# Gate of the feed-forward layers by the Silu table function, with the tokens' rstd moved to the last product

## The chip, the cores and the metric

The kernel runs on one core of a Trainium2 chip. A core has a matrix engine (TensorE; PE in the profile, PEld for its weight loads), a vector engine (VectorE, DVE), a table-function engine (ScalarE, ACT), a general engine (GpSimd, POOL), a sync engine (SP) and 16 DMA engines. Each engine works through its own instructions in order and waits for the others through semaphores. The metric is the device time of one execution in microseconds (us), the median of several executions.

## The reference, cut to what matters

Two hybrid attention layers come first. Then two layers of another kind follow, over 512 tokens of 1024 features, and the change is in their feed-forward parts:

```python
def swiglu(h, w1, w3, w2):
    return (jax.nn.silu(h @ w1) * (h @ w3)) @ w2
...
for l in range(DEPTH):                                   # DEPTH = 2
    x = x + 0.5 * swiglu(rmsnorm(x, ffn1_norm[l]), ffn1_w1[l], ffn1_w3[l], ffn1_w2[l])
    h = rmsnorm(x, mix_norm[l])
    ...                                                  # HGRN2 heads and a multiscale pool: "mix"
    x = x + mem_cross_attention(rmsnorm(x, xa_norm[l]), rmsnorm(mem, mem_norm[l]), ...)
    x = x + 0.5 * swiglu(rmsnorm(x, ffn2_norm[l]), ffn2_w1[l], ffn2_w3[l], ffn2_w2[l])
return rmsnorm(x, final_norm)
```

rmsnorm multiplies each token by rstd = 1 / sqrt(mean(x * x) + 1e-6) and each feature by a gain. The hidden width of a feed-forward part is 2816, which is 22 tiles of 128 features.

## The kernel before, in words

Activations lie feature-major: 128 features on the partitions, the 512 tokens on the free axis, so one activation tile is 128x512 and x is eight tiles. A dense product is three passes of TensorE (`mm3`, L296 to L298) over an exact split of both operands: a leading part ("hi", h) and the rest ("lo", l). Weights come in chunks by DMA (`wraw`); ScalarE copies out the leading part (`whi`, L287) and VectorE subtracts (`wlo`, L288), with two buffers of each. Three PSUM banks called `mm` collect sums of products, and a unit's sum is taken out of its bank ("evacuated") two units later.

The gain of a norm is applied when x is split for the next product: as a tile of x becomes final, `ready` has ScalarE write `xsh` (L262) and VectorE `xsl` (L263). The rstd is not known then. Its sum of squares passes through TensorE (L421) while the first products run, and `rsqrt` makes the value (Ln L440, Exp L441, Square L442 on ScalarE, then L443 and L444 on VectorE). It is multiplied into the products when they are evacuated. So the first evacuation of a stage waits for that chain, which sits in ScalarE's queue between conversions of weights.

A feed-forward part is `ffn`: two halves of 11 hidden tiles, each half w1 and w3 (22 units in turn, evacuated by `ev`), then w2 (8 units, `ev2`). Each evacuation of w1 gives a gate: si = ps * r on VectorE (L886), a clamp on GpSimd (L501), Exp, Ln, Exp on ScalarE (L504 to L506) for the sigmoid, then * r (L888) and the product with the sigmoid (L889) on GpSimd. The w3 product is multiplied with it on VectorE (L893) and split into `hh` and `hl`. There are 4 such parts of 22 gates, so 88 gates in all.

ScalarE holds one set of table functions at a time. A switch is an instruction of its own, ACT_TABLE_LOAD. The setup of this kernel fetches, at L597, a set that has both Ln and Exp, and nothing later needs another.

The stages, in us of the profiled execution: hybrid layers to 770; feed-forward 1 of layer 0 to 1137; mix to 1350; cross attention to 1510; feed-forward 2 to 1880; then for layer 1 to 2250, 2455, 2615 and 2977; the last norm to the end. The program order is made by a queue of units in which later units start before earlier ones are evacuated, and a scheduler (Tile) puts each engine's instructions in order. Work tiles come from a pool ("slot", 34 buffers).

Of the kernel before, what the change touches and what calls it, by code (L numbers as in the profile page):

```python
"""Two hybrid attention layers, then two HGRN2 / pool / cross-attention layers, on one core.

Activations live feature-major: features on the partitions, the 512 tokens on the free axis.
Dense products run on the tensor engine as float32r passes: an operand is split exactly into
a leading part of 12 significant bits and the rest, and three passes carry lead*lead, rest*lead
and lead*rest, which keeps the accuracy of a float32 product.
"""
# [23 lines left out]
EPS = 1e-6  # L31
# [5 lines left out]
# tiles of a tag get their room in program order, so work that runs at its own pace has a tag of its own  # L37
# [18 lines left out]
# engines of the steps that more than one can take: V(ector), P(ool), A(ctivation)  # L56
# [7 lines left out]
# ---------------------------------------------------------------- layout of the inputs (host)  # L64
def _chunks(w, c):
    """[K, M] -> [M/c, 128, K/128, c]"""
    k, m = w.shape
    return np.ascontiguousarray(w.reshape(k // P, P, m // c, c).transpose(2, 1, 0, 3))


def _cols(v):
    """[n*128] -> [128, n]"""
    return v.reshape(-1, P).T
# [37 lines left out]
def _constants():  # L111
    a = np.zeros((P, CONST.n), np.float32)

    def put(name, v):
        o, w = CONST.at[name]
        a[:, o:o + w] = v

    p = np.arange(P)[:, None]
    put("ident", np.eye(P))
    put("ones", 1.0)  # L120
    put("bd", (p // 64 == np.arange(P)[None] // 64))
    u = np.arange(512)[None]
    dist = p + 384 - u
    put("causal", np.where(dist >= 0, 0.0, BIG))
    cnt = ((dist >= 0) & (dist <= 128)) * 1 + ((dist >= 0) & (dist % 4 == 0)) * 1 + ((dist >= 0) & (dist % 16 == 0)) * 1
    put("dil", np.where(cnt > 0, -np.log(np.maximum(cnt, 1)), BIG))
    put("tri", (u >= p))
    put("reset", (u % 64 != 0))
    put("diag", p % 32 == np.arange(32)[None])
    t16 = np.arange(16)[None]  # L130
    put("pool", np.concatenate([1.0 / np.minimum(t16 + 1, w) for w in (2, 4, 8, 16)], 1))
    put("eps", EPS)
    # pairs s, t of 32 tokens in the two halves of a segment of 2 hs tokens
    lev = np.zeros((P, 5, 32), np.float32)
    s, t = np.arange(P)[:, None] % 32, np.arange(32)[None]
    for n, hs in enumerate((16, 8, 4, 2, 1)):
        lev[:, n] = (s // (2 * hs) == t // (2 * hs)) & (s % (2 * hs) < hs) & (t % (2 * hs) >= hs)
    sel = np.zeros((96, 8, P), np.float32)
    for h in range(8):
        for part in range(3):  # L140
            sel[32 * part + h, h] = 1.0
    return a, lev, sel


def _pack(i):
# [5 lines left out]
    # 8 frequencies x 16 blocks of 32 tokens  # L151
# [55 lines left out]
# ---------------------------------------------------------------- the program  # L207
class Prog:
# [9 lines left out]
    # tiles  # L218
# [34 lines left out]
    # exact split of float32 into two float32r parts  # L253
# [19 lines left out]
    def chunk(self, ap, kt, c):  # L273
        """One chunk of a weight: both parts, [128, kt, c]."""
# [17 lines left out]
    def mm3(self, ps, pairs, first=True, last=True):  # L292
        """ps = sum over pairs of (stationary hi, lo), (moving hi, lo)."""
# [6 lines left out]
    class Unit:  # L300
        """Work of the tensor engine in parts that other work can go between; prep loads its weights."""
# [14 lines left out]
    def unit(self, prep, kt, n, pair, evac, wait=2):  # L316
        """One bank of a dense product: the sum over kt pairs of operands."""
# [16 lines left out]
    def dense(self, chunks, kt, c, act, evac, m0=0, n=T, quick=False):  # L334
        """Feature-major product, a unit for every 128 columns of the weight (one bank); quick: the last ones evacuated at once."""
# [11 lines left out]
    def dense_tok(self, chunks, kt, c, act, evac, nb, c0=0):  # L347
        """Token-major product: tokens on the partitions, the weight's columns on the free axis."""
# [9 lines left out]
    def later(self, n, f):  # L358
        """Run f after n more dense units."""
        self.queue.append([n, f])  # L360

    def chain(self, *steps):
        """Steps that hand over between engines, one after each dense unit, so that none waits in its queue."""
        steps[0]()
        if len(steps) > 1:
            self.later(1, lambda: self.chain(*steps[1:]))
# [13 lines left out]
    def parts_of(self, units):  # L380
        """The parts of the units in order, each with its cost; the next unit's weights are loaded ahead."""
# [13 lines left out]
    def weave(self, main, fill, keep=0, lead=0):  # L395
        """Both lists in their order, merged in proportion to their cost; lead of fill's go first, keep last."""
# [14 lines left out]
    # root mean squares  # L411
    def parts(self, sq, hi, n=T, eng=None):
        """The rest of sq beside its leading part hi."""
# [4 lines left out]
    def colsum(self, ps, which, sq, n=T):  # L418
        """ps = which^T sq, which of zeros and minus ones, sq in parts."""
# [16 lines left out]
    def rsqrt(self, ps, n_mean, n=T):  # L436
        """1 / sqrt(-ps / n_mean + EPS): a table value and a Newton step."""
# [9 lines left out]
    class Next:  # L447
        """The operand of the phase after this one, built tile by tile as x gets final."""
# [39 lines left out]
    def norm(self, cur, cols=False, wait=2):  # L488
        """rstd of the tokens, emitted behind the first dense units, which need it only in their evacuation."""
# [8 lines left out]
    def sigmoid(self, x, t, clamp):  # L498
        """t = 1 / (1 + exp(-x)) as exp(-ln(1 + exp(-x))), x held above -40."""
# [10 lines left out]
    def gate(self, ps, r, then):  # L510
        """g = silu(ps * r), then(g)."""
# [5 lines left out]
    # ------------------------------------------------------------ start  # L517
# [50 lines left out]
    def setup_rope(self):  # L568
        """cos and signed sin of the angles, in a dense layout and then in their rows; reduced by multiples of 2 pi in exact parts."""
# [35 lines left out]
    # ------------------------------------------------------------ hybrid layer  # L605
    def qk_tile(self, ps, r, g, rope, done):
        """Head-wise rms norm (two heads a tile), gain, and the rotary part."""
# [33 lines left out]
    def softmax_rows(self, ps, n, mask, P_out):  # L641
        """P_out = softmax of -(ps + mask) along the free axis."""
# [8 lines left out]
    def stack(self, get, st):  # L651
        """Queries and keys of a pair of heads in parts, stacked so that one pass over 128 rows carries two products:
        [qh; qh] and [ql; ql] against [kh; kl]."""
# [18 lines left out]
    def head(self, get, st, hh, h, fox, done):  # L672
        """One head in three stages; rows 64*hh.. of the output bank get it, feature-major."""
# [6 lines left out]
        def scores(i):  # L680
            qh, ql, kk = st[hh]
            n = (i + 1) * P
            # a float32r product at full rate has at least 256 columns
# [34 lines left out]
    def pipeline(self, heads, stacks):  # L718
        """The heads' steps, those of neighbours overlapped; a pair's operands are stacked ahead of it.

        The values of a pair fill the two halves of the tensor engine's columns side by side.
        """
# [18 lines left out]
    def hybrid(self, l, cur, nx):  # L741
# [5 lines left out]
        # tiles: kb 0-3, qb 4-7, ka 8-11, qa 12-15; queries carry -1/8  # L747
# [10 lines left out]
        def ev_va(c, b, ps):  # L758
            # the first 8 columns are the forget gates
# [86 lines left out]
    def forget(self, z):  # L846
        """Running sums of the log forget gates, split into bfloat16 parts."""
# [4 lines left out]
        # log1p(e) = ln(u) + (e - (u - 1)) / u with u = 1 + e  # L852
# [19 lines left out]
    # ------------------------------------------------------------ second block  # L872
    def ffn(self, l, name, cur, nx):
# [4 lines left out]
        for half in range(2):  # L878
# [3 lines left out]
            def ev(m, ps):  # L882
                j, three = divmod(m, 2)
                if not three:
                    s, b = self.s(nm="si"), self.s(nm="sb")
                    nc.vector.tensor_tensor(s, ps, r["r"], op=ALU.mult)  # L886
                    self.sigmoid(s, b, nc.gpsimd)()
                    nc.gpsimd.tensor_tensor(s, s, r["r"], op=ALU.mult)  # L888
                    nc.gpsimd.tensor_tensor(b, b, s, op=ALU.mult)  # L889
# [9 lines left out]

            def ev2(m, ps):  # L900
                nc.vector.scalar_tensor_tensor(self.x[m], ps, 0.5, self.x[m], op0=ALU.mult, op1=ALU.add)  # L901
                if half == 1:
                    self.ready(nx, m)
# [5 lines left out]
    def lower_bound(self):  # L909
        """Per channel of layer 1: lb, 1 - lb and their logs."""  # L910
# [23 lines left out]
    def hgrn_head(self, l, h, f, v, done):  # L934
        """One head as a list of steps, each ready when the one before it is through its engines.

        The decay exp(b_t - b_s), b the running sum of log f, is a product of two factors of at
        most 1 through a token between s and t: for a segment of 2 hs tokens, t in its right and
        s in its left half, that token is the left half's last. Segments of 2 .. 512 tokens
        cover every pair, and the pair t = s has no decay.  # L940
        """
# [29 lines left out]
        def bound():  # L971
            # logaddexp(log lb, log(1 - lb) + log_sigmoid(z)), k = (1 - lb) * sigmoid(-z)
# [19 lines left out]
        def q64():  # L992
            self.on("qe").tensor_tensor(g["qe"], g["qe"], f[4 + h], op=ALU.mult)
            nc.scalar.activation(g["dk"], g["dk"], AF.Exp)
            # decays of whole 64-token chunks, to the middle of 256 and of 512 tokens
# [62 lines left out]
        def exp(n):  # L1058
            nc.scalar.activation(g[f"W{n}"], g[f"W{n}"], AF.Exp)
# [73 lines left out]
    def mix(self, l, cur, nx):  # L1133
# [26 lines left out]
        def ev_gu(m, ps):  # L1160
# [19 lines left out]
            # the mean over the window minus the frame  # L1180
# [35 lines left out]
    def mem_kv(self, l):  # L1216
        """Keys (feature-major) and values (token-major) of the memory, as units."""
# [27 lines left out]
    def cross(self, l, cur, nx):  # L1245
# [64 lines left out]
        # the first units of the last product run between the steps of the last heads  # L1310
# [74 lines left out]
```

## Time and profile before

| what | value |
|---|---|
| time, median of 3 runs | 2998.93 us (2995.76 to 2999.79) |
| span of the profiled execution, first to last instruction | 2992.6 us |
| TensorE busy | 2929.1 us, 98% |
| VectorE busy | 1674.1 us, 56% |
| ScalarE busy | 1406.6 us, 47% |
| GpSimd busy | 745.2 us, 25% |

The profile holds one execution, and its span stands 6.3 us below the median time. Busy is time in which an engine runs instructions that the profile counts; an engine's idle time costs the program only where another engine waits for it.

### The profile page before, as it was taken

Reading aid. Unit: us, or ns where it says so; the run is one execution under the profiler, and the core shown is the slowest. Engines: PE = TensorE matmul, PEld = TensorE weight load, DVE = VectorE, ACT = ScalarE, POOL = GpSimd, SP = SyncE. Lnnn points to the kernel's source line nnn. Section 1 sums busy time; section 2 is a strip of 40 time slices with the busy share of each in tenths; the row PEclk is TensorE's granted clock in tenths of the full one; section 3 lists DMA queues with packets and bytes.
Section 4 is the critical chain, followed back from the end, with each engine's and each line's share of the span. In section 5 each row is a group of like instructions: output and inputs, shape, how many; then the busy total and the mean of one; then the engine's idle time right before and its main releaser. Section 6 shows DMA issues by size and latency. Waiting matters only on the chain.

```text
span 2992.6 us, 39832 instructions
## 1 busy us (share of the span) xinstructions
PE 2929.1 (98%) x15544; PEld 2372.5 (79%) x15544; DVE 1674.1 (56%) x2698; ACT 1406.6 (47%) x2334; POOL 745.2 (25%) x613
## 2 busy tenths in 40 slices
PE   7999999999999999999999999999999999999997
PEld 6777877778788887798888888888888798888886
DVE  7976678766533337785643333433347976643333
ACT  5876467664532434464443233432434654443342
POOL 3101131011331323331032132321323330132231
PEclk9999999999999999999999999999999999999999
DMA  4432233322223232243132323223232242232322
GB/s 159 121 103 82 95 113 94 106 80 94 96 80 107 87 96 89 68 131 99 57 99 79 111 90 99 97 76 111 83 107 83 79 134 85 71 98 79 110 75 76
DMA packets 93436, 284.10 MB, mean 95 GB/s; under 512 B 12656, under 2 KB 13056, under 8 KB 93120
## 3 DMA queue, kind: packets, MB, share of 16 engines
q1 hardware_dynamic: 92928, 281.26, 29.5%
q8 instruction: 122, 2.00, 0.3%
q14 instruction: 66, 0.54, 0.1%
q10 hardware_dynamic: 288, 0.28, 0.0%
q0 software_dynamic: 32, 0.02, 0.0%
HBM read 261.46 MB, written 2.10 MB: 88 GB/s over the span
## 4 chain that ended last, share of the span: by engine, by line
PE 86%; DVE 7%; ACT 2%; issue 1%; POOL 0%; DMA 0%; DVEq 0%; ACTq 0%; POOLq 0%
PE mm L296 27%; PE mm L297 26%; PE mm L298 26%; PE po L712 2%; DVE wlo L288 1%; PE pt L701 1%; PE aux L687 1%; PE aux L421 1%; PE aux L688 1%; PE po L1103 0%; PE aux L296 0%; PE aux L298 0%; PE aux L297 0%; ACT whi L287 0%; DVE hw L1020 0%
## 5 line engine op out<-in xcount | busy, mean ns | idle before, releaser
L296 PE MATMUL mm<-xsh,whi 128*128 128x512 f32 x2304 | 926.9, 403 | 16.9 <-DVE pol L263 8.1
L297 PE MATMUL mm<-xsl,whi 128*128 128x512 f32 x2304 | 910.5, 395 | 8.0 <-DVE xsl L263 7.6
L298 PE MATMUL mm<-xsh,wlo 128*128 128x512 f32 x2304 | 911.2, 396 | 0.0
L287 ACT ACTIVATE whi<-wraw 128x1024 fp32r<-128x1024 f32 (+4 forms) x526 | 498.5, 984 | 572.2 <-PE mm L297 408.0
L288 DVE TENSOR_TENSOR wlo<-wraw,whi 128x1024 fp32r<-128x1024 f32 (+4 forms) x526 | 596.5, 1165 | 110.4 <-ACT whi L287 106.2
L296 PEld LDWEIGHTS mm<-xsh,whi 128*128 128x128 f32 x2304 | 435.6, 189 | 128.4 <-issue 13.1
L297 PEld LDWEIGHTS mm<-xsl,whi 128*128 128x128 f32 x2304 | 435.7, 189 | 108.2 <-DVE xsl L263 14.5
L298 PEld LDWEIGHTS mm<-xsh,wlo 128*128 128x128 f32 x2304 | 435.1, 189 | 101.4 <-DVE wlo L288 0.2
L501 POOL TENSOR_SCALAR sb<-si 128x512 f32<-128x512 f32 x88 | 130.8, 1487 | 770.0 <-DVE si L886 770.0
L433 POOL TENSOR_TENSOR sq<-sq,sq 128x512 f32<-128x512 f32 (+1 forms) x97 | 132.0, 1361 | 722.5 <-ACT sq L430 711.0
L893 DVE TENSOR_TENSOR sb<-mm,sb 128x512 f32<-128x512 f32 x88 | 60.9, 692 | 435.2 <-POOL sb L889 435.2
L297 PE MATMUL mm<-hl,whi 128*128 128x512 f32 x704 | 277.4, 394 | 0.0
L296 PE MATMUL mm<-hh,whi 128*128 128x512 f32 x704 | 277.2, 394 | 0.0
L298 PE MATMUL mm<-hh,wlo 128*128 128x512 f32 x704 | 276.7, 393 | 0.0
L504 ACT ACTIVATE sb<-sb 128x512 f32<-128x512 f32 x88 | 55.8, 634 | 464.1 <-POOL sb L501 464.1
L901 DVE SCALAR_TENSOR_TENSOR x<-mm,x 128x512 f32<-128x512 f32 x64 | 44.3, 692 | 306.7 <-PE mm L298 306.7
L297 PEld LDWEIGHTS mm<-hl,whi 128*128 128x128 f32 x704 | 132.3, 188 | 30.8
L296 PEld LDWEIGHTS mm<-hh,whi 128*128 128x128 f32 x704 | 131.8, 187 | 31.3
L298 PEld LDWEIGHTS mm<-hh,wlo 128*128 128x128 f32 x704 | 132.5, 188 | 30.3
L886 DVE TENSOR_TENSOR si<-mm,rt 128x512 f32<-128x512 f32 x88 | 60.9, 692 | 134.4 <-PE mm L298 134.2
L889 POOL TENSOR_TENSOR sb<-sb,si 128x512 f32<-128x512 f32 x88 | 113.9, 1296 | 67.3 <-ACT sb L506 67.3
L888 POOL TENSOR_TENSOR si<-si,rt 128x512 f32<-128x512 f32 x88 | 114.9, 1306 | 7.3
(360 smaller groups left out, 4580.8 us busy)
## 6 DMA issues: line engine op xcount, KB each, us to landing
wraw<-in_ffn_w_dram SPq DMA_DIRECT2D x176, 512.0 KB
wraw<-in_ffn_w_dram SPq DMA_DIRECT2D x64, 384.0 KB
wraw<-in_ffn_w_dram SPq DMA_DIRECT2D x64, 320.0 KB
z<-z SPq DMA_DIRECT2D x128, 128.0 KB
wraw<-in_w_out_dram SPq DMA_DIRECT2D x32, 512.0 KB
wraw<-in_w_qk_dram SPq DMA_DIRECT2D x30, 512.0 KB
wraw<-in_w_g_dram SPq DMA_DIRECT2D x16, 512.0 KB
wraw<-in_w_gate_dram SPq DMA_DIRECT2D x16, 512.0 KB
```

What stands on the lines that cost most here:

```text
L287: nc.scalar.activation(hi[:, a:b], raw[:, a - o:b - o], AF.Copy)
L288: nc.vector.tensor_tensor(lo[:, a:b], raw[:, a - o:b - o], hi.bitcast(F32)[:, a:b], op=ALU.subtract)
L296: self.nc.tensor.matmul(ps, ah, bh, start=first and i == 0, stop=False)
L297: self.nc.tensor.matmul(ps, ah, bl, start=False, stop=False)
L298: self.nc.tensor.matmul(ps, al, bh, start=False, stop=last and i == n - 1)
L433: (eng or self.on("acc")).tensor_tensor(acc[:, :n], acc[:, :n], sq[:, :n], op=ALU.add)
L501: clamp.tensor_scalar(t, x, -40.0, None, op0=ALU.max)
L712: nc.tensor.matmul(self.po[rows, j * P:], v[j][:, 64 * h:64 * h + 64], ptS[b][:, o:o + T - j * P], start=j == 0, stop=j == 2)
L886: nc.vector.tensor_tensor(s, ps, r["r"], op=ALU.mult)
L888: nc.gpsimd.tensor_tensor(s, s, r["r"], op=ALU.mult)
L889: nc.gpsimd.tensor_tensor(b, b, s, op=ALU.mult)
L893: nc.vector.tensor_tensor(b, ps, b, op=ALU.mult)
```

## The change

The gate becomes one table function, Silu, on ps * r. The w3 product is no longer multiplied by r: since r is one number for each token, it can be applied after w2, where `ev2` adds the product to x. That addition becomes two instructions with a tile between them. The rest of the diff removes comments. The new instructions have lines L887 (Silu), L901 and L902, the product with w3 moves from L893 to L891, and lines behind `ffn` move by one.

```diff
             def ev(m, ps):
                 j, three = divmod(m, 2)
                 if not three:
-                    s, b = self.s(nm="si"), self.s(nm="sb")
-                    nc.vector.tensor_tensor(s, ps, r["r"], op=ALU.mult)
-                    self.sigmoid(s, b, nc.gpsimd)()
-                    nc.gpsimd.tensor_tensor(s, s, r["r"], op=ALU.mult)
-                    nc.gpsimd.tensor_tensor(b, b, s, op=ALU.mult)
+                    b = self.s(nm="sb")
+                    nc.vector.tensor_tensor(b, ps, r["r"], op=ALU.mult)
+                    nc.scalar.activation(b, b, AF.Silu)
                     pend[0] = b
...
             def ev2(m, ps):
-                nc.vector.scalar_tensor_tensor(self.x[m], ps, 0.5, self.x[m], op0=ALU.mult, op1=ALU.add)
+                t = self.s(nm="xr")
+                nc.vector.scalar_tensor_tensor(t, ps, 0.5, r["r"], op0=ALU.mult, op1=ALU.mult)
+                nc.vector.tensor_tensor(self.x[m], t, self.x[m], op=ALU.add)
                 if half == 1:
                     self.ready(nx, m)
```

In the compiled program ScalarE has 84 table loads where it had 4. One stands ahead of the first Silu; from there on, each Ln and each Exp that follows the other kind has one of its own. By stage the 80 new ones are: the first Silu of each feed-forward part, 4 in all; 28 in the mix stage of layer 0 and 36 in that of layer 1; 2 at each start of a cross attention and of the last three feed-forward parts; 2 in the last norm. Two of each mix stage's loads belong to the norm at its start.

ScalarE where feed-forward 2 of layer 0 starts, before (`ry` and `rt` are the rstd in the making, `aux` the sum of squares, the number after a name counts tiles):

```order
1313 L287 ACTIVATE whi_14253<-wraw_14255 128x1024
1314 L440 ACTIVATE ry_14207<-aux_14200,cst_62 128x512
1315 L287 ACTIVATE whi_14253<-wraw_14259 128x1024
1316 L441 ACTIVATE ry_14207<-ry_14207 128x512
1317 L442 ACTIVATE rt_14208<-ry_14207 128x512
1318 L504 ACTIVATE sb_14215<-sb_14215 128x512
```

and with the change:

```order
1300 L287 ACTIVATE whi_14147<-wraw_14149 128x1024
1301 L440 ACT_TABLE_LOAD
1302 L440 ACTIVATE ry_14107<-aux_14100,cst_62 128x512
1303 L287 ACTIVATE whi_14147<-wraw_14153 128x1024
1304 L441 ACT_TABLE_LOAD
1305 L441 ACTIVATE ry_14107<-ry_14107 128x512
1306 L442 ACTIVATE rt_14108<-ry_14107 128x512
1307 L887 ACT_TABLE_LOAD
1308 L887 ACTIVATE sb_14114<-sb_14114 128x512
```

Each step of `rsqrt` that was ready to run has a load ahead of it, and a third load stands ahead of the first Silu (L887).

ScalarE in the mix stage of layer 0, with the change, at one of the gates of the HGRN2 heads (`sg` is its sigmoid; `poh`, `msh` and `sq` belong to the pool and to the memory's norm):

```order
1098 L504 ACTIVATE sg_11640<-sg_11640 128x512
1099 L262 ACTIVATE poh_11650<-mm_11561,prm_61 128x512
1100 L505 ACT_TABLE_LOAD
1101 L505 ACTIVATE sg_11640<-sg_11640,cst_62 128x512
1102 L430 ACTIVATE sq_11868<-mem_11864 128x256
1103 L506 ACT_TABLE_LOAD
1104 L506 ACTIVATE sg_11640<-sg_11640 128x512
```

Before, the same seven steps without the two loads stood there in the same order; now the Ln and the second Exp of each such gate have a load.

VectorE where feed-forward 1 of layer 0 ends, before (`x_12` is the last tile of x, `xsl` its rest part for the next product, `wlo` a weight's rest):

```order
1290 L901 SCALAR_TENSOR_TENSOR x_12_72<-mm_10336,x_12_72 128x512
1291 L288 TENSOR_TENSOR wlo_10424<-wraw_10425,whi_10423 128x1024
1292 L288 TENSOR_TENSOR wlo_10424<-wraw_10429,whi_10423 128x1024
1293 L263 SCALAR_TENSOR_TENSOR xsl_10372<-x_12_72,prm_61,xsh_10371 128x512
1294 L415 TENSOR_TENSOR ql_10461<-sq_10066,qh_10459 128x512
```

and with the change:

```order
1305 L901 SCALAR_TENSOR_TENSOR xr_10268<-mm_10234,rt_8039 128x512
1306 L902 TENSOR_TENSOR x_12_72<-xr_10268,x_12_72 128x512
1307 L288 TENSOR_TENSOR wlo_10324<-wraw_10325,whi_10323 128x1024
1308 L263 SCALAR_TENSOR_TENSOR xsl_10272<-x_12_72,prm_61,xsh_10271 128x512
1309 L288 TENSOR_TENSOR wlo_10324<-wraw_10329,whi_10323 128x1024
1310 L415 TENSOR_TENSOR ql_10361<-sq_9952,qh_10359 128x512
```

The addition (L902) is new. The second half of the weight's rest has moved behind `xsl`.

## Rows read from the trace of the kernel before

**Rows 1.** The profiled page: span, and each engine's busy time, share and instructions.

```profile
span 2992.6 us, 39832 instructions
...
PE 2929.1 (98%) x15544; PEld 2372.5 (79%) x15544; DVE 1674.1 (56%) x2698; ACT 1406.6 (47%) x2334; POOL 745.2 (25%) x613
```

**Rows 2.** Windows: length, busy time (instructions) per engine, clock; first feed-forward stage, mix stage.

```profile
770.00:1137.00 367.00, 366.97 (x1584) 297.23 (x1583) 142.69 (x171) 135.04 (x186) 100.70 (x73) 1.00 0.30 96
1240.00:1290.00 50.00, 42.00 (x355) 33.99 (x354) 44.25 (x80) 31.60 (x60) 14.19 (x17) 0.86 0.22 70
780.00:825.00 45.00, 45.00 (x195) 36.42 (x194) 18.26 (x22) 19.87 (x28) 19.69 (x16) 1.00 0.29 94
860.00:905.00 45.00, 45.00 (x196) 36.40 (x195) 15.41 (x20) 13.79 (x20) 9.46 (x7) 1.00 0.26 81
```

**Rows 3.** Timeline of ScalarE near the start of the program.

```profile
5.17 1.28 ACT L917 ACT_TABLE_LOAD   x1
6.46 0.20 ACT L917 ACTIVATE lb<-lb 128x4 f32<-128x4 f32 x1
...
12.91 1.28 ACT L595 ACT_TABLE_LOAD   x1
17.62 0.23 ACT L595 ACTIVATE rope<-rope 128x32 f32<-128x32 f32 x1 [3.43 <-DVE rope L594]
```

**Rows 4.** Timelines of ScalarE and of weight loads where feed-forward 2 of layer 0 starts.

```profile
1516.42 0.67 ACT L440 ACTIVATE ry<-aux,cst 128x512 f32<-128x512 f32 x1
1516.99 1.05 ACT L287 ACTIVATE whi<-wraw 128x1024 fp32r<-128x1024 f32 x1
1517.94 0.62 ACT L441 ACTIVATE ry<-ry 128x512 f32<-128x512 f32 x1
...
1521.46 0.19 PEld L296 LDWEIGHTS mm<-xsh,whi 128*128 128x128 f32 x1 [0.24 <-DVE si L886]
```

**Rows 5.** Timelines of VectorE and of weight loads where feed-forward 1 of layer 0 ends.

```profile
1128.28 0.69 DVE L901 SCALAR_TENSOR_TENSOR x<-mm,x 128x512 f32<-128x512 f32 x1 [2.66 <-PE mm L298]
1129.18 2.36 DVE L288 TENSOR_TENSOR wlo<-wraw,whi 128x1024 fp32r<-128x1024 f32 x2 [0.22 <-ACT whi L287]
...
1133.31 0.19 PEld L297 LDWEIGHTS mm<-xsl,whi 128*128 128x128 f32 x1 [0.46 <-DVE xsl L263]
```

**Rows 6.** Timeline of TensorE: waits inside the two mix stages.

```profile
1173.48 0.34 PE L1074 MATMUL aux<-hW 128*32 128x32 f32 x8 [3.16 <-ACT ha L232]
...
1246.55 0.79 PE L296 MATMUL mm<-xsh,whi 128*128 128x512 f32 x1 [4.28 <-DVE pol L263]
...
1262.71 0.80 PE L296 MATMUL mm<-xsh,whi 128*128 128x512 f32 x1 [0.72 <-DVE pol L263]
...
2279.41 0.38 PE L1076 MATMUL aux<-hW 128*32 128x32 f32 x12 [2.05 <-ACT ham L1033]
...
2297.71 0.38 PE L1074 MATMUL aux<-hW 128*32 128x32 f32 x22 [0.59 <-DVE hac L1088]
...
2356.44 0.50 PE L296 MATMUL mm<-xsh,whi 128*128 128x512 f32 x1 [3.05 <-DVE pol L263]
...
2391.43 0.38 PE L421 MATMUL aux<-ql,onesR 128*128 128x256 f32 x1 [0.61 <-DVE ql L415]
```

**Rows 7.** Windows of ScalarE alone, one stretch in each mix stage.

```profile
1262.00:1284.30 22.30, 17.77 (x35) 0.85 0.21 66
2367.00:2391.00 24.00, 21.08 (x41) 1.00 0.26 78
```

**Rows 8.** Windows behind two of the waits in the mix stages, all engines.

```profile
1173.40:1176.70 3.30, 3.22 (x38) 2.35 (x38) 3.30 (x9) 1.58 (x4) 0.00 (x0) 0.50 0.24 98
2279.40:2282.80 3.40, 3.39 (x59) 2.65 (x60) 3.40 (x6) 0.76 (x3) 1.45 (x3) 1.00 0.02 5
```

**Rows 9.** Timeline of ScalarE at the end of the program.

```profile
2978.78 0.69 ACT L440 ACTIVATE ry<-aux,cst 128x512 f32<-128x512 f32 x1 [1.32 <-PE aux L421]
2979.50 0.63 ACT L441 ACTIVATE ry<-ry 128x512 f32<-128x512 f32 x1
```

## The prediction

> **What bounds the kernel now.** I read the page first, then windows by stage, then the waits of TensorE and of its weight loads, and last the timelines at the places where those waits fall. The page says that TensorE is busy for 2929.1 of 2992.6 us [rows 1]. So the reader's first question is where the other engines still make it wait, since only there can an edit on ScalarE, GpSimd or VectorE move the end. In the windows the feed-forward stage has TensorE busy for 366.97 of 367.00 us, with ScalarE at 135.04 and GpSimd at 100.70: everything of the old gate lies beside products. A window in the mix stage reads otherwise: TensorE 42.00 of 50.00, VectorE 44.25, ScalarE 31.60, at a clock of 0.86 [rows 2]. There the chains of the HGRN2 heads and of the pool are as long as the products that cover them.
>
> **What the change takes away: 0 us.** Each gate loses two ScalarE and three GpSimd instructions. Their cover is a TensorE that never stops in these stages, so shorter gates leave the products where they are. GpSimd's load could still slow the products beside it. Two windows of 45 us in the same stage hold 195 products with GpSimd busy 19.69 us and 196 with 9.46 us [rows 2]: one product in 195, or 0.5%, is the upper bound of that gain, about 7 us over the four feed-forward stages (4 x 367 us). That is also the grain of the count, so I take 0.
>
> **What it adds on ScalarE.** The compiled order has 80 more table loads, all but four of them far from the Silus: once Silu has thrown out the set that served Ln and Exp alike, each following Ln and Exp is given its own set. A load takes 1.28 us in this trace. It runs when the queue reaches it: one ran at 12.91, and its own activation, which waited for VectorE, came at 17.62, with the ScalarE idle of 3.43 us lying between them [rows 3]. So a load is free where ScalarE would have idled as long, and costs about 1.30 us where its queue is tight (1.4 where it also breaks the overlap of two instructions). The bounds for 80 loads are 0 and 80 x 1.4 = 112 us; the places decide.
>
> The Trainium skill says of a switch, in "ScalarE: Activation LUTs", section "What ACT_TABLE_LOAD costs", that besides the load of about 1.28 us it holds a drain of about 1.38 us. The trace agrees on the first part and shows nothing of the second: the activation behind the load at 5.17 starts at 6.46, when that load ends [rows 3]. By the page each exposed load would come to about 2.66 us, and the sum below would about double; that is rival C.
>
> *Starts of stages: 7 x 2.8 = 19.6 us.* At the start of feed-forward 2, L440, a weight conversion (L287) and L441 stand back to back on ScalarE, and the first evacuation at their end is what the weight loads wait for, 0.24 us late already [rows 4]. There is no slack. Two loads go into this chain, the second behind the conversion, at 1.4 us each. Seven starts have such a pair: two mixes, two cross attentions, three feed-forward parts. The third load, ahead of the first Silu, lies behind the chain and delays a gate only: 0 us.
>
> *Inside the mix: 34 us.* I took each TensorE wait of these stages [rows 6] and counted the loads in the stretch of ScalarE ahead of it, less ScalarE's idle time there. Layer 0: ahead of 1173.48 three loads less 0.8 idle, 3.1 us; ahead of 1246.55 four loads, and VectorE then runs without a pause up to the releaser, so I take 4.1 after a little idle time; two ahead of 1262.71, 2.6; then eight up to 1284.3, 10.4 us, in a window where ScalarE works 17.77 of 22.30 us [rows 7], so 5.9. Layer 1: two exposed and one half hidden ahead of 2279.41, 3.1; two ahead of 2297.71, 2.6; one us of six loads ahead of 2356.44, where products cover the rest; ten up to 2391, 13.0 us against an idle time of 24.00 - 21.08 = 2.92 [rows 7], so 10.1. At the end of each mix another pair stands in the heads' rstd, which is on the way to the last product: 2.6 each. The sum is 18.3 + 19.4 = 37.7. Some of these chains run beside one another, so I keep nine tenths: 34. The bounds are 0 and all 60 loads exposed, 60 x 1.30 = 78.
>
> *Last norm: 2.0 us.* L440 idles 1.32 us ahead of it, which hides its load; L441 follows within 0.03 us, so its load is exposed [rows 9]: 1.3. The extra addition on the last tile of x, 0.69 us by the like instruction of [rows 5], is exposed here too: 0.7.
>
> *Clock: 6 us.* After a TensorE wait of 3.16 us the granted clock is 0.50 over the next 3.3 us, that is 1.2 GHz instead of 2.4; after one of 2.05 us it stays at 1.00 [rows 6, 8]. A new wait at a start is 0.24 + 2.8 = 3.0 us, between the two. A half clock over 3.4 us loses 1.7 us. With seven starts and three or four lengthened waits in the mixes, all of them would cost 18 us, none 0; I take a third.
>
> **What it adds on VectorE: -1.3 us.** There are 64 more additions (L902). 61 of them lie in stretches where VectorE works 142.69 of 367 us, and the bank is freed by L901 as before. On the way to the next stage is the last tile of x, at three boundaries: L901, two conversions of a weight's rest, then `xsl`, for which the weight loads wait 0.46 us [rows 5]. The new order puts the addition in (0.69) but moves one of the two conversions (half of 2.36) behind `xsl`. So `xsl` comes about 0.5 us earlier, and the wait of 0.46 goes: 3 x -0.46, rounded to -1.3. If the conversion's move didn't help, it would be 3 x 0.69 = +2.1; both ends are in the range. Without the slack of VectorE the 64 additions would cost 44 us.
>
> The sum: 19.6 + 34 + 2.0 + 6 - 1.3 = 60.3 us. The profiled execution would have a span of 2992.6 + 60 = 3053 us. The median of the runs is 6.3 us above that span, so I forecast 2998.9 + 60 = 3059 us.
>
> **Rivals.**
>
> A. *The mix hides its loads.* ScalarE is idle for 18 of 50 us even in the dense window [rows 2], and loads run ahead of their operands [rows 3]. Then starts, last norm and a little clock remain: 19.6 + 2.0 + 3 - 1.3 = 23 us, about 3022. Against it: the two windows of rows 7 have no room for eight and ten loads. The chance is 0.14.
>
> B. *Every load is exposed.* 80 x 1.35 = 108 us, with the clock 12 more: about 3119. For it speak the dependent steps Exp, Ln, Exp; against it windows in the mix in which TensorE is fully busy. 0.05.
>
> C. *A load costs more than its row*, by a drain or by the activation behind it starting cold. At twice the price, starts 39, mix 34 x 2 = 68 and more, clock 10: about +120, 3119. The loads seen here show no such tail, but each stood at a quiet place. 0.07.
>
> D. *The other side: faster.* Free GpSimd and fewer ScalarE accesses let the products run closer: 0.5% of 1468 us is 7 us, which decides only if the exposed loads cost less than that. At seven starts without slack two loads alone are past it. About 2992 would come out; 0.03.
>
> E. *The change doesn't do what it says.* If the loads that switch back and forth were nearly free in the run, or the weight loads at the starts waited for something else than I read, the sum falls within 0.2% (6 us, about what a measurement of this kernel can tell from no change). 0.03.
>
> **How the numbers follow.** The forecast's mechanism has 0.68 and spans 3035 to 3090: mix between 20 and 55, clock between 0 and 15. The range for 8 in 10 goes down to rival A's near half, 3024, and up to 3096. Faster 0.03, same 0.03, slower 0.94.
>
> **What the changed profile would show.** 84 ACT_TABLE_LOAD rows of 1.28 us, about 105 us in all, 64 of the new ones in the mixes. At each of the seven starts L886, or what the stage has in its place, comes 2.8 us later, with a wait of about 3 us on the weight loads. The feed-forward stages keep their length apart from their first 10 us; the mix stages are 15 to 20 us longer each, and their windows show ScalarE past 80% where it was 17.77 of 22.30. GpSimd loses most of its 100.70 us in each of the four feed-forward stages with no effect. The prediction is wrong if the mixes keep their length (A), if an activation starts over a microsecond behind its load (C), or if products in the feed-forward windows come closer than 196 in 45 us (D).

## The result, and the profile after

The changed kernel takes 3076.31 us (median of 4 runs, 3071.56 to 3076.97) against 2997.39 us before (4 runs, 2995.76 to 2999.79). The ratio is 1.0262, with a 95% interval of 1.0249 to 1.0275, so the change costs 79 us. The forecast was 3059 us, in a range from 3024 to 3096: the way it went and its mechanism were right. The change was forecast at 60 us and measured 79, so its size was 19 us short.

The page of the changed kernel, which answers to [rows 1]:

```profile
span 3075.2 us, 39448 instructions
...
PE 2956.9 (96%) x15544; PEld 2393.1 (78%) x15544; DVE 1722.2 (56%) x2762; ACT 1395.7 (45%) x2238; POOL 376.7 (12%) x349
```

The reader can split the loss here. TensorE runs the same 15544 products. Its idle time, span less busy time, rose from 63.5 to 118.3 us, by 54.8; its busy time rose by 27.8 us. Two different things happened to it: it waited more, and it ran its products more slowly. ScalarE is a little less busy than before and GpSimd half as busy, and neither helped.

The groups of table loads, over the whole program (count, busy us, mean ns, idle before):

```profile
L440 ACT ACT_TABLE_LOAD x18 | 23.1, 1283 | 0.3
L441 ACT ACT_TABLE_LOAD x17 | 21.8, 1283 | 0.3
L958 ACT ACT_TABLE_LOAD x12 | 15.4, 1283 | 0.2
```

Each load is the 1.28 us of [rows 3], and the largest groups belong to the rstd and the HGRN2 gates, not to Silu.

The start of feed-forward 2 in layer 0, timeline of ScalarE and then of the weight loads, which answers to [rows 4]:

```profile
1549.45 1.28 ACT L440 ACT_TABLE_LOAD   x1
1550.75 0.69 ACT L440 ACTIVATE ry<-aux,cst 128x512 f32<-128x512 f32 x1
1551.33 1.05 ACT L287 ACTIVATE whi<-wraw 128x1024 fp32r<-128x1024 f32 x1
1552.40 1.28 ACT L441 ACT_TABLE_LOAD   x1
1553.70 0.63 ACT L441 ACTIVATE ry<-ry 128x512 f32<-128x512 f32 x1
1554.36 0.63 ACT L442 ACTIVATE rt<-ry 128x512 f32<-128x512 f32 x1
1555.01 1.28 ACT L887 ACT_TABLE_LOAD   x1
1557.20 1.23 ACT L887 ACTIVATE sb<-sb 128x512 f32<-128x512 f32 x2 [0.91 <-DVE sb L886]
...
1557.22 0.19 PEld L296 LDWEIGHTS mm<-xsh,whi 128*128 128x128 f32 x1 [3.06 <-DVE sb L886]
```

The chain from L440 to L442 has two loads more, one ahead of L440 and one ahead of L441, and ScalarE has no idle time between its steps. The wait of the weight loads grew from 0.24 to 3.06 us, by 2.82. The third load, ahead of Silu, is over before Silu's operand is there (its idle time of 0.91 us ends with L886): it costs nothing.

The end of feed-forward 1, timelines of VectorE and GpSimd, which answer to [rows 5]; first two lines of the kernel before:

```profile
1131.38 1.33 POOL L433 TENSOR_TENSOR sq<-sq,sq 128x512 f32<-128x512 f32 x1 [6.31 <-ACT sq L430]
1131.46 1.80 DVE L263 SCALAR_TENSOR_TENSOR xsl<-x,prm,xsh 128x512 fp32r<-128x512 f32 x1
```

and in the changed kernel:

```profile
1132.58 0.69 DVE L901 SCALAR_TENSOR_TENSOR xr<-mm,rt 128x512 f32<-128x512 f32 x1 [2.17 <-PE mm L298]
1133.31 0.69 DVE L902 TENSOR_TENSOR x<-xr,x 128x512 f32<-128x512 f32 x1
1133.92 1.22 DVE L288 TENSOR_TENSOR wlo<-wraw,whi 128x1024 fp32r<-128x1024 f32 x1
1135.06 0.75 DVE L263 SCALAR_TENSOR_TENSOR xsl<-x,prm,xsh 128x512 fp32r<-128x512 f32 x1
1135.62 1.35 POOL L433 TENSOR_TENSOR sq<-sq,sq 128x512 f32<-128x512 f32 x1 [6.28 <-ACT sq L430]
1135.73 2.32 DVE L288 TENSOR_TENSOR wlo<-wraw,whi 128x1024 fp32r<-128x1024 f32 x1
```

`xsl` is done 3.2 us after L901 began; before it took 5.0 (1128.28 to 1133.26). The addition went in and the conversion went behind, and the wait of 0.46 us is gone. More than half of the 1.8 us that `xsl` gains comes from `xsl` itself, which took 1.80 us before and 0.75 after. Before, it started beside the GpSimd product L433; now the second conversion does, and it takes 2.32 us where the first takes 1.22. It is so at all three boundaries. That the GpSimd product is what lengthens the VectorE instruction beside it was not tested here.

The feed-forward stage and its window of 45 us, all engines, which answer to [rows 2]:

```profile
773.78:1140.78 367.00, 367.00 (x1583) 297.46 (x1582) 153.65 (x186) 107.14 (x142) 9.20 (x7) 1.00 0.28 96
...
783.70:828.70 45.00, 45.00 (x196) 36.43 (x195) 18.01 (x21) 12.65 (x16) 0.00 (x0) 1.00 0.27 94
```

GpSimd is silent in that window, and TensorE does 196 products where it did 195. The relief bought nothing.

The loss sits in the mixes. Windows over the same work, from the end of feed-forward 1 to the start of the cross attention, in the kernel before:

```profile
1142.00:1349.50 207.50, 195.77 (x1928) 168.42 (x1927) 163.50 (x306) 106.36 (x184) 74.77 (x89) 0.96 0.29 94
2252.00:2456.00 204.00, 195.87 (x1943) 167.71 (x1943) 176.99 (x326) 113.59 (x195) 78.46 (x89) 0.99 0.31 99
```

and in the changed kernel:

```profile
1145.92:1379.56 233.64, 202.60 (x1928) 173.00 (x1927) 161.94 (x306) 143.42 (x213) 73.54 (x89) 0.92 0.25 84
2292.16:2528.86 236.70, 207.09 (x1943) 176.30 (x1943) 179.15 (x326) 160.42 (x231) 76.57 (x89) 0.94 0.26 85
```

The two mixes hold the same 1928 and 1943 products and are 58.8 us longer: 40.8 us more idle time of TensorE (from 19.86 to 60.65 us) and 18.0 us more busy time, at clocks of 0.92 and 0.94 where they were 0.96 and 0.99. Some of the waits, which answer to [rows 6]:

```profile
1182.37 0.37 PE L1075 MATMUL aux<-hW 128*32 128x32 f32 x9 [4.14 <-ACT ha L232]
1260.76 0.80 PE L296 MATMUL mm<-xsh,whi 128*128 128x512 f32 x1 [5.63 <-DVE pol L263]
...
1303.61 0.58 PE L297 MATMUL mm<-msl,whi 128*128 128x256 f32 x1 [3.82 <-DVE msl L263]
...
1309.91 0.58 PE L421 MATMUL aux<-qh,onesR 128*128 128x256 f32 x1 [3.81 <-ACT qh L469]
...
2431.84 0.79 PE L296 MATMUL mm<-xsh,whi 128*128 128x512 f32 x1 [4.45 <-DVE pol L263]
...
2448.77 0.39 PE L297 MATMUL mm<-msl,whi 128*128 128x256 f32 x1 [1.94 <-DVE msl L263]
```

The old waits are longer by 1.0 to 1.4 us (3.16 to 4.14, 4.28 to 5.63, 3.05 to 4.45), and there are new ones in the stretches that held eight and ten loads (1303.61 and 1309.91, 2448.77).

### The profile page after: what moved, and what is told of

The parts are those of the page before. It is cut to its first block, busy times and chain, and to the rows that moved or that the text cites. A ratio compares the mean times of both kernels' runs of the same rounds, so it can differ in the third digit from the quotient of the medians.

```text
span 3075.2 us, 39448 instructions
## 1 busy us (share of the span) xinstructions
PE 2956.9 (96%) x15544; PEld 2393.1 (78%) x15544; DVE 1722.2 (56%) x2762; ACT 1395.7 (45%) x2238; POOL 376.7 (12%) x349
## 4 chain that ended last, share of the span: by engine, by line
PE 82%; DVE 7%; ACT 6%; issue 2%; POOL 0%; DMA 0%; DVEq 0%; ACTq 0%; POOLq 0%
PE mm L296 25%; PE mm L297 25%; PE mm L298 25%; PE po L712 1%; DVE wlo L288 1%; ACT whi L287 1%; PE pt L701 1%; PE aux L687 1%; PE aux L688 1%; PE aux L421 1%; ACT L441 1%; ACT L440 1%; PE po L1104 0%; ACT L958 0%; ACT ry L440 0%
## 5 line engine op out<-in xcount | busy, mean ns | idle before, releaser
L288 DVE TENSOR_TENSOR wlo<-wraw,whi 128x1024 fp32r<-128x1024 f32 (+4 forms) x526 | 604.3, 1178 | 138.3 <-ACT whi L287 126.1
L433 POOL TENSOR_TENSOR sq<-sq,sq 128x512 f32<-128x512 f32 (+1 forms) x97 | 125.8, 1297 | 1981.9 <-ACT sq L430 1964.7
L891 DVE TENSOR_TENSOR sb<-mm,sb 128x512 f32<-128x512 f32 x88 | 60.9, 692 | 410.0 <-PE mm L298 409.7
L887 ACT ACTIVATE sb<-sb 128x512 f32<-128x512 f32 x88 | 55.5, 632 | 326.8 <-DVE sb L886 326.8
L901 DVE SCALAR_TENSOR_TENSOR xr<-mm,rt 128x512 f32<-128x512 f32 x64 | 44.3, 692 | 264.6 <-PE mm L298 264.6
L886 DVE TENSOR_TENSOR sb<-mm,rt 128x512 f32<-128x512 f32 x88 | 60.6, 691 | 144.4 <-PE mm L298 144.3
L262 ACT ACTIVATE xsh<-x,prm 128x512 fp32r<-128x512 f32 x96 | 68.5, 715 | 113.7 <-DVE x L1211 32.2
L263 DVE SCALAR_TENSOR_TENSOR xsl<-x,prm,xsh 128x512 fp32r<-128x512 f32 x96 | 99.3, 1034 | 29.3 <-ACT xsh L262 29.1
L296 PE MATMUL mm<-whi,xsh 128*128 128x256 f32 (+1 forms) x384 | 114.2, 297 | 0.0
```

Source lines behind the costliest of these rows:

```text
L262: self.nc.scalar.activation(hi[:, :n], src, AF.Copy, scale=g)
L263: self.nc.vector.scalar_tensor_tensor(lo[:, :n], src, g, hi.bitcast(F32)[:, :n], op0=ALU.mult, op1=ALU.subtract)
L288: nc.vector.tensor_tensor(lo[:, a:b], raw[:, a - o:b - o], hi.bitcast(F32)[:, a:b], op=ALU.subtract)
L296: self.nc.tensor.matmul(ps, ah, bh, start=first and i == 0, stop=False)
L433: (eng or self.on("acc")).tensor_tensor(acc[:, :n], acc[:, :n], sq[:, :n], op=ALU.add)
L886: nc.vector.tensor_tensor(b, ps, r["r"], op=ALU.mult)
```

## The experiments

Theory 1: the loss is the alternation of sets between Ln and Exp, wherever it falls on the path, and neither Silu nor the moved rstd. Theory 2: the moved rstd with its 64 additions, or Silu itself, carries a good part.

**The set put back.** One load of the Ln and Exp set behind the last Silu of each part.

```diff
             self.go(self.dense([w13[NH * half + i] for i in range(NH)], KD, 256, xs, ev))
             self.flush()
+            if half == 1:
+                self.tc.keep_in_program_order(nc.scalar.preload_act_table_set("natural_log_exp_and_others"))
```

> The changed kernel with one load of the Ln and Exp set put behind the last Silu of each feed-forward part, so that 12 table loads stand in the program and not 84. Theory 1 (the 79 us are the loads between Ln and Exp, whatever the Silus and the moved rstd do): the time comes back to that of the kernel before, 2994 to 3000 us, the three waits of 0.46 us for xsl gone, and 8 more loads that nobody waits for. Theory 2 (the moved rstd and its additions, or the Silus themselves, cost a good part): 3015 us or more.

Measured: 2996.67 us (11 runs), before 2995.93 on the same chips; ratio 1.0001, 0.9992 to 1.0010. Four loads are put in, the program has 72 fewer in all, and the loss is gone. Silu and the moved rstd are in it, so theory 2 falls.

**Silu alone.**

```diff
                     nc.scalar.activation(b, b, AF.Silu)
+                    nc.gpsimd.tensor_tensor(b, b, r["r"], op=ALU.mult)
...
-                t = self.s(nm="xr")
-                nc.vector.scalar_tensor_tensor(t, ps, 0.5, r["r"], op0=ALU.mult, op1=ALU.mult)
-                nc.vector.tensor_tensor(self.x[m], t, self.x[m], op=ALU.add)
+                nc.vector.scalar_tensor_tensor(self.x[m], ps, 0.5, self.x[m], op0=ALU.mult, op1=ALU.add)
```

> The Silu gate alone: the rstd stays in the gate (a product on GpSimd behind the Silu) and the last addition is that of before. 84 table loads. Theory 1: as the changed kernel, 3070 to 3080 us, perhaps 1 us above it for the waits on xsl that come back. Theory 2: near 3000 if the moved rstd was the cost, between if both were.

Measured: 3071.95 us, ratio 1.0252 (1.0238 to 1.0266). The interval overlaps that of the whole change: Silu's arrival is enough for all of it.

**The moved rstd alone.** The kernel before with the new `ev2`, and without the product of the gate with r (L888).

```diff
                     self.sigmoid(s, b, nc.gpsimd)()
-                    nc.gpsimd.tensor_tensor(s, s, r["r"], op=ALU.mult)
                     nc.gpsimd.tensor_tensor(b, b, s, op=ALU.mult)
...
-                nc.vector.scalar_tensor_tensor(self.x[m], ps, 0.5, self.x[m], op0=ALU.mult, op1=ALU.add)
+                t = self.s(nm="xr")
+                nc.vector.scalar_tensor_tensor(t, ps, 0.5, r["r"], op0=ALU.mult, op1=ALU.mult)
+                nc.vector.tensor_tensor(self.x[m], t, self.x[m], op=ALU.add)
```

> The moved rstd alone: the gate keeps Exp, Ln, Exp, and the set of before stays in ScalarE. Theory 1: 2995 to 3000 us, the waits for xsl of 0.46 us shorter or gone at three boundaries, 0.7 us more at the last norm, so 0 to 1 us faster than before. Theory 2: 10 us or more slower, by 64 additions of 0.69 us on VectorE.

Measured: 2997.16 us, ratio 1.0006 (0.9998 to 1.0015). No change that can be measured; the tenths of a microsecond at the boundaries are too small for these runs.

**The gate left out.**

```diff
-                    s, b = self.s(nm="si"), self.s(nm="sb")
-                    nc.vector.tensor_tensor(s, ps, r["r"], op=ALU.mult)
-                    self.sigmoid(s, b, nc.gpsimd)()
-                    nc.gpsimd.tensor_tensor(s, s, r["r"], op=ALU.mult)
-                    nc.gpsimd.tensor_tensor(b, b, s, op=ALU.mult)
+                    b = self.s(nm="sb")
+                    nc.vector.tensor_tensor(b, ps, r["r"], op=ALU.mult)
```

> The kernel before with the sigmoid left out of the feed-forward gates (the gate is the product of the two halves times the rstd, once), so that ScalarE loses 3 and GpSimd 3 instructions a gate and no table load comes in; the output is another function. If a gate is hidden work, as the prediction took it, the time stays within 0.2%: 2992 to 3001 us, and a feed-forward window of 45 us keeps its 195 to 196 products. If GpSimd's and ScalarE's traffic slowed the products, the time falls by 7 us or more, to 2990 or below.

Measured: 2995.77 us, ratio 0.9999 (0.9990 to 1.0008). Even with no sigmoid at all there is nothing to gain in these stages: the gate is hidden work. Its first window of 45 us holds 196 products.

**Loads at the starts alone, without Silu.** The kernel before with a load ahead of L440 and of L441 at the seven starts; the lines that set `extra` there are left out.

```diff
+        if self.extra:
+            self.tc.keep_in_program_order(nc.scalar.preload_act_table_set("natural_log_exp_and_others"))
         nc.scalar.activation(y[:, :n], ps[:, :n], AF.Ln, bias=self.cst("eps"), scale=-1.0 / n_mean)
+        if self.extra:
+            self.tc.keep_in_program_order(nc.scalar.preload_act_table_set("natural_log_exp_and_others"))
         nc.scalar.activation(y[:, :n], y[:, :n], AF.Exp, scale=-0.5)
```

> The kernel before with two more loads of the set that is already there, ahead of the Ln and of the Exp of the rstd, at the seven starts of stages of the second block (not at the first feed-forward part): 14 loads, no Silu, no moved rstd. Theory 1 (no slack at a start, a load costs its row of 1.28 us and what it breaks of the overlap): 2.6 to 2.9 us a start, so 18 to 20 us over before, about 3015 us, up to 3020 with a half clock behind some starts. The rival with a drain behind each load: about 37 us, 3033. The rival that starts have slack: under 5 us.

Measured: 3009.08 us, ratio 1.0043 (1.0028 to 1.0058), so 12.9 us, less than expected. The order in the trace explains it: the first load of the pair came to stand ahead of the weight conversion, where ScalarE then idles 4.72 us, and only the second was exposed. Each start moved by about 1.90 us. That is more than 1.28 us because in this build the second conversion came to stand between L441 and L442: at the start of feed-forward 2 of layer 0 its subtraction on VectorE ends at 1523.01, behind L442 (1522.26), and the next step of `rsqrt`, on VectorE too, has to wait for it. Two loads at a start thus cost 1.9 us here and 2.8 us in the changed kernel, by where they stand.

**Only the first feed-forward parts' set put back.** `set_back` with `name == "ffn1"` in the condition.

> The changed kernel with the Ln and Exp set put back behind the Silus of the two first feed-forward parts only, so that both mixes, both cross attentions and both second feed-forward parts run on one set; 14 loads, of which the pair at the start of layer 1's first feed-forward part and the pair of the last norm are left exposed. Theory 1: 3 us for that start and 1 to 2 us for the last norm over before, 2999 to 3002 us.

Measured: 3002.08 us, ratio 1.0019 (1.0010 to 1.0029). The 5.9 us are just above the 4 to 5 us that were expected. In the trace the one exposed start costs 4.3 us by the same products, 2.6 of waiting and 1.6 by products at half clock behind it; the rest of the 7.0 us between the two spans lies at the last norm.

**Loads in the mixes alone.** The condition with `name == "ffn2"`, and one more load of the set behind the heads of the mix, ahead of its output product.

> The complement: the changed kernel with the set put back behind the second feed-forward parts and at the end of each mix, so that only the two mixes, their starts included, have loads between Ln and Exp; 76 loads. By the difference of the two traces, 53 us inside the mixes and 6 us at their two starts less 1 us at the ends of feed-forward parts: about 3053 us. By the sum of the prediction (34 inside, 6 at starts, 4 of clock) 3040. With the kernel mix_back it must add up to the changed kernel, short of 11 to 12 us for the four starts that both spare.

Measured: 3054.49 us, ratio 1.0194 (1.0177 to 1.0211), 58.3 us over before. The mixes carry three quarters of the loss, as the windows said, and the 44 us that come from the prediction's terms are too few. With the 5.9 us of the run before and 11 to 12 for the four starts that both spare, the sum is 75 to 76 us, some 3 short of the 79.

**Loads at the HGRN2 gates.** The kernel before with a load ahead of the Ln and of the second Exp of `sigmoid` in the mix.

> The kernel before with a load ahead of the Ln and of the second Exp of the eight HGRN2 gates in the mixes, 16 loads. Six of them lie in each of the stretches for which the prediction took loads less idle time. By that count, 6 x 1.30 less 4.5 and less 2.9 us of idle time: 3.3 and 4.9, about 8 us over before, 3004. If the idle time moves along, since the work that ScalarE waits for there waits for ScalarE's own results, and the overlap of neighbours is lost: 6 x 1.38 in each, 16 us, with a longer half clock up to 20, so 3012 to 3016.

Measured: 3016.70 us, ratio 1.0070 (1.0055 to 1.0085): 20.5 us for 16 loads. That is above both expectations (3004, and 3012 to 3016) and looks like 1.28 us each, but it can't be read so: the loads changed the scheduler's order, and 337 of TensorE's 15544 products are not the ones that stood at their place before. Inconclusive on the idle time.

**Waits of three lengths.** By then the open question was the slower products. Two and four loads, to another set and back once or twice, were put between L440 and L441, at the same seven starts, without Silu. The edit for four (for two it has 1 in place of 2; the lines that set `extra` are left out):

```diff
         nc.scalar.activation(y[:, :n], ps[:, :n], AF.Ln, bias=self.cst("eps"), scale=-1.0 / n_mean)
+        for st in 2 * ("trig_and_small", "natural_log_exp_and_others") if self.extra else ():
+            self.tc.keep_in_program_order(nc.scalar.preload_act_table_set(st))
         nc.scalar.activation(y[:, :n], y[:, :n], AF.Exp, scale=-0.5)
```

> The kernel before with two table loads between the Ln and the Exp of the rstd at the same seven starts, so that none of them can run ahead in ScalarE's idle time. If the second load of a start costs its row, 1.90 + 1.28 = 3.2 us a start, 22 us over before, nearly all of it idle time of TensorE. For the clock: in the changed kernel three of the seven starts, with waits of 2.6 us, are followed by a half clock; if waits of this length bring it at random, two to four of them here, 1.3 us each, so TensorE's busy time rises by 3 to 5 us and the time is 3019 to 3025.

> The same with four loads in that place: 1.90 + 3 x 1.28 = 5.7 us a start, 40 us of idle time. If a longer wait always brings the half clock, all seven starts are followed by it, for 3.4 to 6.8 us, and TensorE's busy time rises by 9 to 18 us over before: 3045 to 3055 us. If the clock falls by chance whatever the length, busy time rises by 3 to 5 us as with two loads: 3039 to 3042.

Measured: 3025.53 us with two (1.0098, 1.0083 to 1.0113) and 3044.46 us with four (1.0165, 1.0148 to 1.0182). TensorE's busy time is 2939.2 and 2943.4 us, 10 and 14 over the kernel before. The time with two is just above its range, for which the busy time was to rise by 3 to 5 us; 2 of its 10 us lie in the hybrid layers, which the edit doesn't touch. The time with four is just under its range; the mix of layer 0 took 4.5 us of the first delay back. Windows of TensorE alone just behind three of the waits with two loads (length, busy time, clock):

```profile
1413.69:1415.69 2.00, 2.00 (x6) 0.50 0.09 35
1534.58:1536.58 2.00, 2.00 (x11) 1.00 0.08 31
1904.92:1906.92 2.00, 2.00 (x7) 0.50 0.08 33
```

and with four loads:

```profile
1414.49:1416.49 2.00, 2.00 (x5) 0.50 0.29 115
1538.47:1540.47 2.00, 2.00 (x5) 0.50 0.29 113
1913.93:1915.93 2.00, 2.00 (x5) 0.50 0.36 147
```

In 2 us TensorE begins 11 products at clock 1.00, which is 2.4 GHz, and 5 to 7 at 0.50, which is 1.2 GHz. Over all seven starts: with waits of 1.7 us (`start_loads`) none is followed by the half clock, with 2.6 us (the changed kernel) three, with 3.0 us four, with 5.5 us all seven. By the same products in two traces, a start that is followed by it has 1.6 to 1.8 us more busy time in the changed kernel and with two loads, and a start that is not has 0.2.

The timeline of ScalarE with four loads settles the price of one:

```profile
1527.58 0.67 ACT L442 ACTIVATE ry<-aux,cst 128x512 f32<-128x512 f32 x1
1528.27 5.15 ACT L444 ACT_TABLE_LOAD   x4
1533.42 0.63 ACT L445 ACTIVATE ry<-ry 128x512 f32<-128x512 f32 x1
```

Four loads take 5.15 us, and the Exp starts at their end and takes 0.63 us, as without a load ahead of it (0.62 in [rows 4]).

## Why the prediction was right, and where it was short

**Taken away: 0 us.** Right. Leaving the sigmoid out altogether changes nothing.

**Seven starts at 2.8 us.** Right: 2.82 us at the start shown, and 2.83 to 2.86 us at three others, when the same product is looked up in both traces; the remaining three waited as long and were followed by the half clock, which is another term. `start_loads` shows the condition: a load that may run ahead in idle time is free.

**Inside the mix, 34 us.** As a count of waiting, right. The idle time of TensorE in the mixes rose by 40.8 us; two of the starts are in it, 2.6 us each, which leaves 35.5. Place by place it was less exact. By the same products in both traces, the wait grew by 1.0 us at 1173.48 and 0.7 at 2279.41, where 3.1 were counted for each; by 2.9 at 2356.44, where one was; and by 6.9 around 1284, where 5.9 were. These errors largely cancel, so that the sum comes out within 2 us is partly luck. With the half clock, which is another term, 11 us were lost around 1284.

**Last norm and boundaries.** The waits at the boundaries went, and 0.3 us came back at each, so 1.0 us was gained where 1.3 were put down (3 x 0.46 is 1.4). `xsl` came 1.8 us earlier and not 0.5, but no more than the wait was there to win. From the last product of feed-forward 2 (2975.16 before, 3054.98 after) to the end the changed kernel lost 2.8 us, against 2.0: the last tile of x came 1.2 us later where 0.7 were counted, the load ahead of L441 cost 1.3 as counted, and 0.3 are two products at half clock.

**All waiting together** was forecast at 19.6 + 34 + 2.0 - 1.3 = 54.3 us. The trace shows 54.8 us more idle time, which is closer than the parts are.

**Clock: 6 us.** This term was mis-sized: it measured 27.8 us more busy time for the same products. 18.0 of it lie in the mixes. There I counted three or four lengthened waits, but the loads lengthened more waits and made new ones, and the half clock stayed longer than 3.4 us behind some of them. Behind the wait that ended at 1303.61 it stayed for 13.65 us (window of TensorE):

```profile
1303.64:1317.29 13.65, 9.34 (x67) 0.50 0.21 70
```

So even the upper end of this term, 18 us with every counted wait followed by the half clock, was too low. 4.8 us lie in the hybrid layers, which the change doesn't touch, and the rest in the other stages, most of it at the starts. The part in the hybrid layers is chance of one execution, so 23.0 us are left for the change, against 6. The same wait there, in the kernel before and then in the changed one, and the window behind it:

```profile
763.46 0.50 PE L297 MATMUL mm<-xsl,whi 128*128 128x512 f32 x1 [1.63 <-DVE xsl L263]
...
765.60:768.60 3.00, 3.00 (x14) 1.00 0.06 15
```

```profile
765.82 0.50 PE L297 MATMUL mm<-xsl,whi 128*128 128x512 f32 x1 [1.61 <-DVE xsl L263]
...
768.00:771.00 3.00, 3.00 (x9) 0.50 0.05 14
```

So of the 82.6 us between the two spans, some 4 to 5 are not the change's, which fits the 79 us between the medians. That the clock follows from the length of a wait is shown in part: more of the longer waits were followed by the half clock. What decides a single case stays open; a wait of 1.6 us had it here, and seven of 1.7 us in another kernel had not. In the profiled executions of the ten experiments, whose hybrid layers are the same, that wait (1.5 to 1.7 us) was never followed by it.

**The signs.** The loads, the starts and GpSimd came out as the prediction said. ScalarE, at 17.77 of 22.30 and 21.08 of 24.00 us before [rows 7], is nearly full in the same two stretches of the changed kernel:

```profile
1277.50:1306.00 28.50, 26.47 (x40) 0.86 0.14 51
2420.00:2457.00 37.00, 36.00 (x53) 0.87 0.13 45
```

But the mixes are 26 and 33 us longer, not 15 to 20 each, since the clock's part fell there. And 84 loads of 1.28 us are 108 us of ScalarE's time, not about 105; no term rests on that.

**The rivals.** A (the mix hides its loads) falls with the windows of the mixes and with `mix_loads`. B (every load exposed, 108 us of waiting) falls with the 54.8 us of idle time. C, a load that costs more than its row, falls with the four loads in 5.15 us. The Trainium skill gives a drain of about 1.38 us for each switch ("ScalarE: Activation LUTs", section "What ACT_TABLE_LOAD costs"); that row shows none on the path here, and the measurement decides. D falls with `no_gate`, E with the result.

No version was found that beats both kernels: with the set put back, the changed kernel equals the one before.

## What to carry to other kernels

A function from a new table set is paid for by the code that runs after it: look where the next Ln and Exp get their tables, and put the shared set back by one load behind the last use of the new one. Of a load's 1.28 us only what can't run ahead of a waiting activation counts, so count loads in the stretches of ScalarE that end in a wait of TensorE. Then add a second price, since a TensorE that waits longer also runs at half clock more often behind the wait: here 23 us on top of 54.8, once the share of the untouched hybrid layers is taken off.

## What was not expected of the hardware

With the same seven waits lengthened, the half clock came behind 0, 3, 4 and 7 of them at 1.7, 2.6, 3.0 and 5.5 us. And relief of GpSimd, from 19.69 to 0.00 us in a window of 45 us, left TensorE's products as they were (195 and 196). And the VectorE instruction that starts beside GpSimd's L433 is longer at each of three boundaries: 1.80 us for `xsl` where it takes 0.75 apart from it, 2.32 for a conversion where it takes 1.22. The cause was not tested.
